# ConvGLU gate chunks and Mamba-2 convolution chunks projected in token rows and turned through HBM

## The chip, the cores and the metric

The kernel runs on one core of one Trainium2 chip. The metric is the device time of one execution in microseconds; lower is better. The time before is the median of three runs. The engines that matter are TensorE (PE, with its weight loads as PEld), VectorE (DVE), ScalarE (ACT) and GpSimd (POOL); SyncE (SP) and GpSimd also issue the transfers.

## The reference, cut to what matters

One layer over 256 tokens with a width of 2048, all in float32. Each sub-layer normalises its input and adds its result to the residual.

```python
proj = u @ w_in                                  # HGRN2, z, xbc, dt and two output gates
xbc = silu(causal_dwconv(xbc_raw, conv_w, conv_b))      # kernel width 4, 8 groups of 256+128+128 channels
xs, bm, cm = split(xbc)                          # then the Mamba-2 scan, gated by silu(z), normed
merged = sigmoid(g_hg) * y_hg + sigmoid(g_m2) * y_m2    # then w_out
# cross-attention into 256 memory tokens
gate, up = split(u @ w_up)                       # 5632 channels each
gate = causal_dwconv(gate, conv_w, conv_b)       # kernel width 3
h = h + (gelu(gate) * up) @ w_down               # then a last RMSNorm
```

A causal convolution runs along the tokens, separately for each channel. It is therefore wanted with channels on the partitions and tokens along the free dimension.

## The kernel before, in words

Every weight matrix is streamed from HBM once, in pieces of 128 x 2048 float32 (1 MB). `order` (lines 87 to 107) lists the pieces in the order of their use. `weights()` (line 201) hands out the next piece, and before that it advances every generator in `background` by one step and sees to it that three pieces are on their way. `issue()` loads a piece through SyncE's queue and splits it by halves of 1024 columns: ScalarE rounds a half to `hi` (line 130) and VectorE forms the rest `lo` (line 131). `hi` and `lo` have five buffers each, `raw` three. Activations are held as hi and lo parts side by side too, so a product is three matmuls: hi by hi, hi by lo, lo by hi.

There are two ways to use a piece.

- `project` (line 238) makes a chunk of 128 output channels for all 256 tokens. The weight is the stationary operand. For each of the 16 blocks of the inner dimension there is one matmul of `hi` over 512 columns (both parts of the activation) and one of `lo` over 256 columns, 32 matmuls for 1 MB. The result has channels on the partitions in two parts, which `join` (line 261) adds: a ScalarE copy out of PSUM and a VectorE sum.
- `project_tok` (line 245) makes 512 output channels for all tokens from four pieces. The activation is the stationary operand, and 24 matmuls of 512 columns use 1 MB. The result has tokens on the partitions, in two PSUM banks of 128 tokens each.

PSUM has four banks for these results (`pj`), two for `lev` and two for `misc`.

Results in token rows are turned by VectorE and HBM: VectorE transposes squares of 32 x 32 (`V.transpose`), `to_squares` (line 307) writes the four partition blocks to HBM with four GpSimd transfers, and one more transfer reads them back with channels on the partitions. The tokens then stand in another order, which `in_order` (line 323) undoes as a view.

Work that is not a projection runs in generators. Each `yield` ends a step, and a step belongs to one piece of weights. Their matmuls keep their place in the program order (`mm`, line 80); other instructions are placed by the scheduler of the tile framework when their operands and buffers are free. A tile name has a fixed number of buffers, and a new tile waits until an old one of that name has had its last use.

The parts around the change:

- Mamba-2, `m2_project` (line 715) and `m2_scan` (line 733). For each of eight groups four chunks are projected with `project(s2)`, joined into `raw` (name `t`, one buffer), and convolved by VectorE in four instructions into `sz` (two buffers). The scan of the group is then put in the background; it pauses one step (even group) or three (odd), applies SiLU, turns x, computes the decays, the product of B and C, the output, the gating and the norm, and writes the group's rows of `ym`. Every second group also has a gate projection of four pieces ahead of it (`m2_gates`).
- The feed-forward stage (lines 1047 to 1081). `values()` projects four chunks of `up` in token rows and turns them (`ut`, two buffers of four chunks). It runs four chunks ahead of the gate. Each of the 44 gate chunks is projected with `project(u3)`, joined, multiplied by the norm factor `r_f`, convolved in three instructions, put through Gelu, multiplied by `r_f` and by the turned value, and split into `hid[c]`. ScalarE's queue carries 16 small transfers of the residual in between.
- The down projection (from line 1090) uses seven matmul blocks in place of eight for some pieces, for which VectorE and ScalarE prepare sums of weights (`seven_forms`) and of inputs (`input_forms`).

Of the kernel before, what the change touches and what calls it, by code (L numbers as in the profile page):

```python
# [9 lines left out]
F32 = mybir.dt.float32  # L10
# [4 lines left out]
ALU = mybir.AluOpType  # L15
# [4 lines left out]
P = 128  # L20
T = 256
D = 2048
# [20 lines left out]
NS = 6  # L43

# [20 lines left out]
def hybrid_trunk(ctx, tc, xT, memT, par, cst, msk, w_k0, w_ka, w_va, w_hg, w_hv, w_hog, w_ghg, w_bhg, w_dt,  # L65
                 w_z, w_m2, w_gm2, w_bm2, w_out, w_q, w_o, w_ug, w_uv, w_dn, fin_g, outT):
    nc = tc.nc
# [125 lines left out]
    def pause(n):  # L193
        for _ in range(n):
            yield True
# [149 lines left out]
    def pc(name, i=0, n=1):  # L345
        o, _ = PCOLS[name]
        return par_t[:, o + i:o + i + n]
# [356 lines left out]
    def m2_chunk(g, i):  # L704
        return 2 * g + i if i < 2 else (16 + g if i == 2 else 24 + g)
# [9 lines left out]
    def m2_project(g):  # L715
        sz = mp.tile([P, 4, T], F32, name="sz", bufs=2)
        cb = mp.tile([P, 4, T], F32, name="vc", bufs=2)
        nc.sync.dma_start(out=cb, in_=cum_d[4 * g:4 * g + 4, :].partition_broadcast(P))
        for i in range(4):
            c = m2_chunk(g, i)  # L720
            ps = project(s2)
            raw = mp.tile([P, T], F32, name="t", bufs=1)
            join(mp, ps, raw)
            o = sz[:, i, :]
            V.tensor_scalar(out=o, in0=raw, scalar1=pc("m2_cw", 4 * c + 3), scalar2=pc("m2_cb", c),
                            op0=ALU.mult, op1=ALU.add)
            for s in range(1, 4):
                V.scalar_tensor_tensor(out=o[:, s:T], in0=raw[:, 0:T - s],  # L728
                                       scalar=pc("m2_cw", 4 * c + 3 - s), in1=o[:, s:T],
                                       op0=ALU.mult, op1=ALU.add)  # L730
        return sz, cb

    def m2_scan(g, sz, cb, zt):
        yield from pause(1 + 2 * (g % 2) if g else 0)

# [310 lines left out]

    def values():

        yq = fu.tile([P, 1024], F32, name="yq", bufs=1)
        for q, ps in enumerate(project_tok(u3)):  # L1050
            V.transpose(out=yq.rearrange("p (n q r) -> p q n r", q=2, r=B)[:, q],  # L1051
                        in_=ps.rearrange("p (n c) -> p n c", c=B))
        yd = to_squares(yq, 16, "u_d")
        ut = fu.tile([P, 4, T], F32, name="ut", bufs=2)
        G.dma_start(out=ut, in_=yd.rearrange("(j p) t -> p j t", p=P))
        return ut

    uts = [values()]
    for c in range(KF):
        if c % 4 == 0 and c + 4 < KF:  # L1060
            uts.append(values())
        if c % 2 == 0 and 4 <= c < 36:
            b, n = (c - 4) // 4, (c - 4) // 2 % 2 * (D // 2)
            nc.scalar.dma_start(
                out=rows_d[b * B:(b + 1) * B, n:n + D // 2].rearrange("i (n c) -> i n c", c=B),
                in_=h2_sq[:, n // B:n // B + D // 2 // B, b * B:(b + 1) * B])
        ps = project(u3)
        g = fu.tile([P, T], F32, name="g", bufs=1)
        join(fu, ps, g)
        V.tensor_tensor(out=g, in0=g, in1=r_f, op=ALU.mult)  # L1070
        gc = fu.tile([P, T], F32, name="gc", bufs=2)
# [6 lines left out]
        V.tensor_tensor(out=gc, in0=gc, in1=r_f, op=ALU.mult)  # L1078
        gv = gc.rearrange("p (q b t) -> p q b t", q=2, t=B)
        V.tensor_tensor(out=gv, in0=gv, in1=in_order(uts[c // 4][:, c % 4, :]), op=ALU.mult)  # L1080
        split(hid[c], gc)
    fx.close()

# [169 lines left out]
def _layout(inp):  # L1253
# [5 lines left out]
    swap = np.arange(D).reshape(GROUPS, 2, P // B, B).transpose(0, 2, 1, 3).ravel()  # L1259
    xs = _cols(cut(10240, 2048)).reshape(GROUPS, 2, P, 2048)  # L1260
    b = _cols(cut(12288, 1024))[:, None]
    c = _cols(cut(13312, 1024))[:, None]
    dt = np.zeros((D, P), f)
# [3 lines left out]
    k0 = ka[:NS].reshape(NS, P, KD // 2, 2, P).transpose(2, 1, 3, 0, 4)  # L1267
    up = inp["ffn_w_up"][0]
    out = _cols(inp["w_out"][0])
# [10 lines left out]
    def put(name, a):  # L1280
# [34 lines left out]
        "w_bhg": _toks(inp["w_branch_hg"][0]), "w_dt": _cols(dt),  # L1315
        "w_z": _toks(cut(8192, 2048)[:, swap]), "w_m2": np.concatenate([xs, b, c], 1), "w_gm2": _toks(cut(16416, 2048)),
        "w_bm2": _toks(inp["w_branch_m2"][0]), "w_out": out,
        "w_q": _cols(inp["xa_wq"][0]), "w_o": _cols(inp["xa_wo"][0]),
        "w_ug": _cols(up[:, :FF]), "w_uv": _toks(up[:, FF:]),
        "w_dn": np.ascontiguousarray(dn.transpose(0, 1, 3, 2, 4)).reshape(2, KF // 2, P, 2048),  # L1320
# [20 lines left out]
```

## Time and profile before

| | |
|---|---|
| median of three runs | 2229.68 us (2229.58 to 2229.78) |
| the profiled execution | 2230.02 us |
| its span, first to last instruction | 2228.3 us |
| mean granted TensorE clock | 0.998 |
| moved from and to HBM | 445.20 MB read, 25.20 MB written |

Busy time by stretch of the span, in us:

| stretch | what runs | TensorE | VectorE | ScalarE | GpSimd |
|---|---|---|---|---|---|
| 0 to 170 | memory keys, norms | 167.88 | 125.31 | 109.48 | 1.25 |
| 170 to 548 | HGRN2 | 378.00 | 320.09 | 274.27 | 40.77 |
| 548 to 711 | first Mamba-2 group, HGRN2 branch | 163.00 | 87.50 | 81.31 | 6.35 |
| 711 to 995 | Mamba-2 groups | 284.00 | 224.57 | 192.61 | 64.00 |
| 995 to 1132 | gates, Mamba-2 branch | 137.00 | 84.22 | 65.34 | 24.38 |
| 1132 to 1220 | output projection | 88.00 | 63.57 | 52.97 | 0.00 |
| 1220 to 1418 | cross-attention | 198.00 | 128.71 | 111.93 | 12.20 |
| 1418 to 1513 | its output projection | 94.83 | 71.98 | 54.67 | 0.00 |
| 1513 to 2000 | gate and up | 487.00 | 345.09 | 257.35 | 37.09 |
| 2000 to 2124 | down, first part | 124.00 | 109.96 | 69.64 | 0.00 |
| 2124 to 2229 | down, second part, last norm | 95.63 | 79.78 | 51.59 | 0.00 |

Busy time is the time covered by an engine's instructions. Matmuls overlap, so the cost of one is read from the distance between the starts of neighbours and not from its own duration. A row of a group of instructions gives line, engine, operation, output and inputs, count, then total busy time and mean duration of one in ns, then the idle time of the engine just before them and what ended it. A row of a timeline gives start and duration in us and, after `x`, how many instructions are merged in it.

### The profile page before, as it was taken

What the parts mean: (1) busy time and instruction counts of PE and PEld (TensorE: products, weight loads), DVE (VectorE), ACT (ScalarE), POOL (GpSimd) and SP (SyncE); (2) the same over time, 40 slices, a digit from 0 to 9 for tenths busy, and PEclk for the clock granted to TensorE, in tenths of its full rate; (3) what the DMA queues carried; (4) which work ended last, traced back from release to release, by engine and by line L of the source; (5) the groups of instructions that cost most, each with busy time, mean ns of one, the idle gap of its engine ahead of it and who ended that gap; (6) DMA issues with size and microseconds to landing.
All of it is one profiled execution on the core that took longest, in us unless ns stands there. A gap on an engine that the chain in (4) does not pass through costs nothing.

```text
span 2228.3 us, 32921 instructions
## 1 busy us (share of the span) xinstructions
PE 2217.3 (100%) x12620; PEld 1890.7 (85%) x12620; DVE 1640.8 (74%) x2660; ACT 1321.2 (59%) x2056; POOL 186.0 (8%) x314
## 2 busy tenths in 40 slices
PE   9999999999999999999999999999999999999998
PEld 8888888888888888888888888888888888888887
DVE  8858888887645779874676766675776776699887
ACT  7567777776545577665456655554554555465554
POOL 0000100110000122220200010001000100100000
PEclk9999999999999999999999999999999999999999
DMA  8655555555655667766676654578666666655654
GB/s 307 235 187 195 184 181 181 182 186 189 228 189 201 225 234 236 229 213 219 228 247 217 219 203 174 180 226 250 214 210 211 225 214 218 213 200 211 220 205 161
DMA packets 100270, 470.45 MB, mean 211 GB/s; under 512 B 29424, under 2 KB 34064, under 8 KB 51088
## 3 DMA queue, kind: packets, MB, share of 16 engines
q1 hardware_dynamic: 69600, 432.36, 54.8%
q0 software_dynamic: 13584, 33.57, 5.3%
q10 hardware_dynamic: 16928, 2.42, 0.6%
q8 instruction: 99, 1.62, 0.3%
q14 instruction: 59, 0.48, 0.1%
HBM read 445.20 MB, written 25.20 MB: 211 GB/s over the span
## 4 chain that ended last, share of the span: by engine, by line
PE 99%; DMA 0%; ACT 0%; SPq 0%; DVE 0%; issue 0%; DVEq 0%; ACTq 0%
PE proj L82 90%; PE misc L82 5%; PE lev L82 4%; DMA raw<-in_w_k 0%; ACT misc L1204 0%; DVE h L1202 0%; PE lev L869 0%; SPq L402 0%; ACT hi L386 0%; SPq L401 0%; DVE c L1221 0%; SPq L405 0%; DVEq L1337 0%; ACT jt L263 0%; PE misc L697 0%
## 5 line engine op out<-in xcount | busy, mean ns | idle before, releaser
L131 DVE TENSOR_TENSOR lo<-raw,hi 128x1024 fp32r<-128x1024 f32 x738 | 896.5, 1222 | 458.8 <-ACT hi L130 425.9
L130 ACT CAST hi<-raw 128x1024 fp32r<-128x1024 f32 x737 | 771.9, 1051 | 546.5 <-PE proj L82 513.0
L82 PE MATMUL proj<-hi,s 128*128 128x512 f32 x2922 | 913.6, 390 | 0.0
L82 PE MATMUL proj<-s,hi 128*128 128x512 f32 x2736 | 645.1, 391 | 1.1 <-ACT hi L386 1.1
L82 PEld LDWEIGHTS proj<-hi,s 128*128 128x128 f32 x2922 | 548.4, 188 | 114.4 <-issue 0.7
L82 PEld LDWEIGHTS proj<-s,hi 128*128 128x128 f32 x2736 | 506.5, 188 | 101.8 <-ACT hi L386 1.6
L82 PE MATMUL proj<-lo,s 128*128 128x512 f32 x1461 | 568.8, 389 | 0.0
L82 PEld LDWEIGHTS proj<-s,lo 128*128 128x128 f32 x2736 | 345.3, 191 | 11.3 <-ACT s L278 0.8
L82 PE MATMUL proj<-s,lo 128*128 128x256 f32 x2736 | 351.6, 283 | 0.2 <-ACT s L278 0.2
L82 PEld LDWEIGHTS proj<-lo,s 128*128 128x128 f32 x1461 | 274.4, 188 | 55.7
L312 POOL DMA_DIRECT2D x_d<-yq x120 | 69.9, 589 | 372.2 <-DVE yq L320 365.6
L165 ACT CAST hi<-raw 128x1024 fp32r<-128x1024 f32 (+1 forms) x56 | 52.1, 944 | 55.0 <-DVE raw L174 35.1
L263 ACT COPY jt<-proj 128x256 f32<-128x256 f32 x123 | 45.6, 371 | 57.5 <-PE proj L82 56.8
L312 POOL DMA_DIRECT2D u_d<-yq x44 | 28.6, 656 | 535.9 <-DVE yq L1051 342.6
L312 POOL DMA_DIRECT2D y_d<-yq x64 | 35.1, 555 | 384.1 <-DVE sm L618 263.1
L166 DVE TENSOR_TENSOR lo<-raw,hi 128x1024 fp32r<-128x1024 f32 (+1 forms) x56 | 60.2, 1088 | 6.9 <-ACT hi L165 6.2
L1074 DVE SCALAR_TENSOR_TENSOR gc<-g,par_t,gc 128x255 f32<-128x255 f32 x88 | 42.4, 482 | 8.7 <-ACT gc L1072 6.0
L728 DVE SCALAR_TENSOR_TENSOR sz<-t,par_t,sz 128x255 f32<-128x255 f32 (+2 forms) x96 | 45.6, 475 | 1.4
L1072 ACT ACTIVATE gc<-g,par_t 128x256 f32<-128x256 f32 x44 | 26.4, 601 | 20.9 <-DVE g L1070 20.9
L82 PE MATMUL proj<-hi,ha 128*128 128x512 f32 x104 | 36.6, 389 | 0.0
L572 DVE TENSOR_TENSOR e<-e,kq 128x256 f32<-128x256 f32 x96 | 34.4, 418 | 0.0
L559 DVE TENSOR_TENSOR e<-bb 128x256 f32<-128x256 f32 x96 | 33.8, 419 | 0.1
(315 smaller groups left out, 1801.3 us busy)
## 6 DMA issues: line engine op xcount, KB each, us to landing
raw<-in_w_uv SPq DMA_DIRECT2D x44, 1024.0 KB, 4.9
raw<-in_w_ug SPq DMA_DIRECT2D x44, 1024.0 KB, 4.8
raw<-in_w_dn SPq DMA_DIRECT2D x44, 1024.0 KB, 4.8
raw<-in_w_hg SPq DMA_DIRECT2D x32, 1024.0 KB, 4.8
raw<-in_w_m SPq DMA_DIRECT2D x32, 1024.0 KB, 5.0
raw<-in_w_hv SPq DMA_DIRECT2D x16, 1024.0 KB, 4.9
raw<-in_w_hog SPq DMA_DIRECT2D x16, 1024.0 KB, 4.8
raw<-in_w_ghg SPq DMA_DIRECT2D x16, 1024.0 KB, 4.8
```

Of the source, the lines that this page charges most:

```text
L82: ins = PE.matmul(*args, **kwargs)
L130: S.copy(out=hi[:, c - a:d - a], in_=raw[:, c:d])
L131: V.tensor_tensor(out=lo[:, c - a:d - a], in0=raw[:, c:d], in1=hi[:, c - a:d - a].bitcast(F32), op=ALU.subtract)
L165: S.copy(out=hi[:, 0:d - c], in_=raw[:, c:d])
L166: V.tensor_tensor(out=lo[:, 0:d - c], in0=raw[:, c:d], in1=hi[:, 0:d - c].bitcast(F32), op=ALU.subtract)
L263: S.copy(out=tmp, in_=ps[:, T:2 * T])
L312: G.dma_start(out=yd.rearrange("(n i) (b f) -> b i n f", i=B, b=P // B)[b], in_=yq[b * B:(b + 1) * B, :].rearrange("i (n f) -> i n f", n=n))
L559: V.tensor_tensor(out=lev[hw].rearrange("p (n c i) -> p n c i", c=2, i=hw), in0=free(bb, 0, [(2 * hw, nb), (T + hw, 2), (1, hw)]), in1=fre ...
L572: V.tensor_tensor(out=ev, in0=ev, in1=free(kq, 0, [(2 * hw, nb), (T + hw, 2), (1, hw)]), op=ALU.mult)
L728: V.scalar_tensor_tensor(out=o[:, s:T], in0=raw[:, 0:T - s], scalar=pc("m2_cw", 4 * c + 3 - s), in1=o[:, s:T], op0=ALU.mult, op1=ALU.add)
L1072: S.activation(out=gc, in_=g, func=AF.Identity, bias=pc("f_cb", c), scale=pc("f_cw", 3 * c + 2))
L1074: V.scalar_tensor_tensor(out=gc[:, s:T], in0=g[:, 0:T - s], scalar=pc("f_cw", 3 * c + 2 - s), in1=gc[:, s:T], op0=ALU.mult, op1=ALU.add)
```

## The change

Both convolved projections go over to token rows.

In the feed-forward stage ten rounds each project 512 value channels and 512 gate channels with `project_tok`, transpose both and write both to HBM (`rows_out`). A generator `four` reads gates and values of a round back by four transfers, one step after it was put in the background, pauses three steps and then handles one chunk in each step. The chunk's first product reads the turned gate through `in_order` in place of the join. The last four gate chunks stay in the direct form, and their four value chunks now use it too: each pair is two `project` calls with a join each. The order of the weights is changed to match (ten times four value and four gate pieces, then four pairs).

In the Mamba-2 part groups 1 to 6 project their four chunks with one `project_tok`, transpose them, write them to HBM and read them back into `sz` with GpSimd transfers. `m2_scan` for these groups first pauses three steps, then copies each chunk out of `sz` into `raw` in token order on ScalarE and convolves it back into `sz`, two chunks a step, then pauses one step (even group) or three (odd). Group 0 and group 7 stay direct; group 7 pauses six steps in place of three. The host's weight layouts follow; they are not shown.

```diff
+FG = 10
...
-    for p in range(-1, KF // 4):
-        order += [w_uv[p + 1, i] for i in range(4) if p + 1 < KF // 4]
-        order += [w_ug[4 * p + i] for i in range(4) if p >= 0]
+    order += [w[p, i] for p in range(FG) for w in (w_uv, w_ug) for i in range(4)]
+    order += [w_ut[c, i] for c in range(KF - 4 * FG) for i in range(2)]
...
         nc.sync.dma_start(out=cb, in_=cum_d[4 * g:4 * g + 4, :].partition_broadcast(P))
+        if 0 < g < GROUPS - 1:
+            pss = project_tok(s2)
+            for j in range(2):
+                yq = mp.tile([P, 2 * T], F32, name="yq", bufs=2)
+                for q in range(2):
+                    V.transpose(out=yq.rearrange("p (n q r) -> p q n r", q=2, r=B)[:, q],
+                                in_=pss[q][:, j * T:(j + 1) * T].rearrange("p (n c) -> p n c", c=B))
+                yd = to_squares(yq, T // B, "r_d")
+                G.dma_start(out=sz[:, 2 * j:2 * j + 2, :], in_=yd.rearrange("(i p) t -> p i t", p=P))
+            return sz, cb
         for i in range(4):
-            c = m2_chunk(g, i)
             ps = project(s2)
             raw = mp.tile([P, T], F32, name="t", bufs=1)
             join(mp, ps, raw)
...
+            convolve(g, sz, i, raw)
...
     def m2_scan(g, sz, cb, zt):
-        yield from pause(1 + 2 * (g % 2) if g else 0)
+        if 0 < g < GROUPS - 1:
+            yield from pause(3)
+            for i in range(4):
+                raw = mp.tile([P, T], F32, name="t", bufs=1)
+                S.copy(out=raw.rearrange("p (q b t) -> p q b t", q=2, t=B), in_=in_order(sz[:, i, :]))
+                convolve(g, sz, i, raw)
+                if i % 2:
+                    yield True
+        yield from pause((0, 1, 3, 6)[0 if g == 0 else 3 if g + 1 == GROUPS else 1 + g % 2])
...
+    def four(p, vd, gd):
+        yield True
+        vts, gts = [], []
+        for j in range(2):
+            for name, d, ts in (("gt", gd, gts), ("vt", vd, vts)):
+                t = fu.tile([P, 2, T], F32, name=name, bufs=2)
+                G.dma_start(out=t, in_=d[j * T:(j + 1) * T, :].rearrange("(i p) t -> p i t", p=P))
+                ts.append(t)
+        yield from pause(3)
+        for i in range(4):
+            c = 4 * p + i
+            g = fu.tile([P, T], F32, name="g", bufs=1)
+            V.tensor_tensor(out=token_order(g), in0=in_order(gts[i // 2][:, i % 2, :]),
+                            in1=token_order(r_f), op=ALU.mult)
+            gc = gated(c, g)
+            V.tensor_tensor(out=token_order(gc), in0=token_order(gc),
+                            in1=in_order(vts[i // 2][:, i % 2, :]), op=ALU.mult)
+            split(hid[c], gc)
+            if i < 3:
+                yield True
...
+    for p in range(FG):
+        residual_rows(2 * p)
+        vd = rows_out("v_d")
+        residual_rows(2 * p + 1)
+        background.append(four(p, vd, rows_out("g_d")))
+    for c in range(4 * FG, KF):
+        ps = project(u3)
+        g = fu.tile([P, T], F32, name="g", bufs=1)
+        join(fu, ps, g)
+        V.tensor_tensor(out=g, in0=g, in1=r_f, op=ALU.mult)
+        gc = gated(c, g)
+        ps = project(u3)
+        up = fu.tile([P, T], F32, name="yq", bufs=1)
+        join(fu, ps, up)
+        V.tensor_tensor(out=gc, in0=gc, in1=up, op=ALU.mult)
         split(hid[c], gc)
+    drain()
```

`rows_out` is `values` without the load: `project_tok(u3)`, two transposes, `to_squares`. `gated` holds the convolution, Gelu and the product with `r_f` as they were; `convolve` holds the four instructions that were in `m2_project`; `residual_rows` holds the residual's transfers, two for each round from the second to the ninth.

More of the change, by code (lines that the diff above doesn't have):

```diff
@@ L65, in hybrid_trunk @@
 def hybrid_trunk(ctx, tc, xT, memT, par, cst, msk, w_k0, w_ka, w_va, w_hg, w_hv, w_hog, w_ghg, w_bhg, w_dt,
[L66 removed]
+                 w_z, w_m2, w_gm2, w_bm2, w_out, w_q, w_o, w_ug, w_uv, w_ut, w_dn, fin_g, outT):
     nc = tc.nc
@@ L723, in m2_project, with convolve @@
             join(mp, ps, raw)
[L724 to L730, printed above, removed]
-        return sz, cb
-    def m2_scan(g, sz, cb, zt):
-        yield from pause(1 + 2 * (g % 2) if g else 0)
+            convolve(g, sz, i, raw)
+        return sz, cb
+    def convolve(g, sz, i, raw):
+        c = m2_chunk(g, i)
+        o = sz[:, i, :]
+        V.tensor_scalar(out=o, in0=raw, scalar1=pc("m2_cw", 4 * c + 3), scalar2=pc("m2_cb", c),
+                        op0=ALU.mult, op1=ALU.add)
+        for s in range(1, 4):
+            V.scalar_tensor_tensor(out=o[:, s:T], in0=raw[:, 0:T - s],
+                                   scalar=pc("m2_cw", 4 * c + 3 - s), in1=o[:, s:T],
+                                   op0=ALU.mult, op1=ALU.add)
+    def m2_scan(g, sz, cb, zt):
+        if 0 < g < GROUPS - 1:
[7 more added lines that the diff above has]
+        yield from pause((0, 1, 3, 6)[0 if g == 0 else 3 if g + 1 == GROUPS else 1 + g % 2])
         xc = mp.tile([P, 2 * T], F32, name=("w", "ql")[g % 2], bufs=1)
@@ L1045, in hybrid_trunk, with rows_out @@
     h2_sq = h2_d.rearrange("n (b i) t -> i (n b) t", i=B)
-    def values():
+    def rows_out(name):
         yq = fu.tile([P, 1024], F32, name="yq", bufs=1)
@@ L1052, in values, with token_order, gated @@
                         in_=ps.rearrange("p (n c) -> p n c", c=B))
[L1053 to L1070, printed above, removed]
+        return to_squares(yq, 16, name)
+    def token_order(x):
+        return x.rearrange("p (q b t) -> p q b t", q=2, t=B)
+    def gated(c, g):
         gc = fu.tile([P, T], F32, name="gc", bufs=2)
@@ L1078, in hybrid_trunk, with residual_rows @@
         V.tensor_tensor(out=gc, in0=gc, in1=r_f, op=ALU.mult)
-        gv = gc.rearrange("p (q b t) -> p q b t", q=2, t=B)
-        V.tensor_tensor(out=gv, in0=gv, in1=in_order(uts[c // 4][:, c % 4, :]), op=ALU.mult)
+        return gc
+    def four(p, vd, gd):
[18 more added lines that the diff above has]
+                yield True
+    def residual_rows(i):
+        if 2 <= i < 18:
+            b, n = (i - 2) // 2, i % 2 * (D // 2)
+            nc.scalar.dma_start(
+                out=rows_d[b * B:(b + 1) * B, n:n + D // 2].rearrange("i (n c) -> i n c", c=B),
+                in_=h2_sq[:, n // B:n // B + D // 2 // B, b * B:(b + 1) * B])
+    for p in range(FG):
[13 more added lines that the diff above has]
+        V.tensor_tensor(out=gc, in0=gc, in1=up, op=ALU.mult)
         split(hid[c], gc)
+    drain()
     fx.close()
@@ L1259, in _layout @@
     swap = np.arange(D).reshape(GROUPS, 2, P // B, B).transpose(0, 2, 1, 3).ravel()
-    xs = _cols(cut(10240, 2048)).reshape(GROUPS, 2, P, 2048)
-    b = _cols(cut(12288, 1024))[:, None]
-    c = _cols(cut(13312, 1024))[:, None]
+    xbc = np.concatenate([cut(10240, 2048).reshape(D, GROUPS, 256),
+                          cut(12288, 1024).reshape(D, GROUPS, P),
+                          cut(13312, 1024).reshape(D, GROUPS, P)], 2).reshape(D, GROUPS * 512)
+    m2 = _toks(xbc)
+    for g in (0, GROUPS - 1):
+        m2[g] = _cols(xbc[:, g * 512:(g + 1) * 512])
     dt = np.zeros((D, P), f)
@@ L1267, in _layout @@
     k0 = ka[:NS].reshape(NS, P, KD // 2, 2, P).transpose(2, 1, 3, 0, 4)
-    up = inp["ffn_w_up"][0]
+    up, up_to = inp["ffn_w_up"][0], FG * 512
     out = _cols(inp["w_out"][0])
```

5 lines of the change are left out of this document (3 added, 2 removed).

## The prediction

> **What bounds the kernel now.** I read the page's busy times first, then the chain that ended last, then what TensorE waited for.
>
> ```profile
> PE 2217.3 (100%) x12620; PEld 1890.7 (85%) x12620; DVE 1640.8 (74%) x2660; ACT 1321.2 (59%) x2056; POOL 186.0 (8%) x314
> PE 99%; DMA 0%; ACT 0%; SPq 0%; DVE 0%; issue 0%; DVEq 0%; ACTq 0%
> ```
> ```profile
> PE proj L82 <- ACT hi L386: 1.1, 2, 0.8
> PE misc L82 <- POOL eps_t L343: 1.0, 1, 1.0
> PE proj L82 <- ACT s L278: 0.2, 1, 0.2
> ```
> TensorE is 99% of the chain, and its waits for other engines add up to 2.3 us, all of them small. So the time is the sum of its matmuls, and a change gains only by making that sum shorter and loses only by making TensorE wait. Where the other engines wait, they wait for it:
>
> ```profile
> ACT hi L130 <- PE proj L82: 513.0, 400, 3.4
> DVE lo L131 <- ACT hi L130: 425.9, 347, 4.4
> ```
> ScalarE casts a weight half (`hi`) as soon as TensorE gives a buffer back, VectorE makes `lo` behind it.
>
> **What the two forms cost on TensorE.** The timeline of TensorE over one period of the feed-forward stage, four gate chunks (`project`) and four megabytes of values (`project_tok`, elided):
>
> ```profile
> 1548.64 2.08 PE L82 MATMUL proj<-s,lo 128*128 128x256 f32 x16
> 1550.56 7.44 PE L82 MATMUL proj<-s,hi 128*128 128x512 f32 x32
> 1557.84 4.00 PE L82 MATMUL proj<-s,lo 128*128 128x256 f32 x32
> 1561.67 7.44 PE L82 MATMUL proj<-s,hi 128*128 128x512 f32 x32
> 1568.95 2.08 PE L82 MATMUL proj<-s,lo 128*128 128x256 f32 x16
> 1570.86 0.40 PE L82 MATMUL proj<-hi,s 128*128 128x512 f32 x1
> ...
> 1592.65 2.08 PE L82 MATMUL proj<-s,lo 128*128 128x256 f32 x16
> ```
> By starts, four gate chunks take 1570.86 - 1548.64 = 22.22 us, four value weights 1592.65 - 1570.86 = 21.79 us. Both stream the same number of columns: `project` 16 x 512 + 16 x 256 for each megabyte, `project_tok` 24 x 512. The difference sits in the 256-wide matmuls: 1561.67 - 1557.84 = 3.83 us for 32 is 0.120 us each, while a 512-wide one of the token form takes 21.79 / 96 = 0.227, so its half would be 0.1135. Sixteen times 0.006 is most of the 0.1075 us by which one megabyte is cheaper in token rows.
>
> [...] The rows above have 0.107, and I take the rows.
>
> **What is moved between the forms.** 40 gate chunks and 24 convolved chunks (six groups of four) go from `project` to `project_tok`. The last four value chunks go the other way, since the remainder of four has a gate and a value weight each in `project`. Net 64 - 4 = 60 megabytes: 60 x 0.1075 = 6.45 us less TensorE work. Other rows bound it: the chain's pieces of one weight,
>
> ```profile
> 881.93 5.47 PE proj L82 x24
> 887.40 1.50 PE misc L82 x16
> ...
> 916.69 0.65 PE misc L82 x4
> 917.34 5.56 PE proj L82 x32
> 922.90 1.50 PE misc L82 x16
> ```
> give 5.56 - 5.47 = 0.09 (5.4 us), and the down stage's 24-matmul weight at 0.68 us for three, 5.44, gives 0.12 (7.2 us):
>
> ```profile
> 2016.16 0.68 PE lev L82 x3
> ```
> **Other work in the feed-forward stage.** The groups of instructions, by shape:
>
> ```profile
> L131 DVE TENSOR_TENSOR lo<-raw,hi 128x1024 fp32r<-128x1024 f32 x738 | 896.5, 1222 | 458.8 <-ACT hi L130 425.9 <-PE proj L82 28.1 <-ACT sq L290 0.4
> L264 DVE TENSOR_TENSOR g<-proj,jt 128x256 f32<-128x256 f32 x44 | 18.4, 418 | 0.1
> L1051 DVE STREAM_TRANSPOSE yq<-proj 128x512 f32<-128x512 f32 x22 | 14.5, 694 | 2.4 <-PE proj L82 2.4
> L320 DVE STREAM_TRANSPOSE yq<-lf 128x256 f32<-128x256 f32 x16 | 7.1, 445 | 2.3 <-ACT lf L645 1.5
> L312 POOL DMA_DIRECT2D u_d<-yq x44 | 28.6, 656 | 535.9 <-DVE yq L1051 342.6 <-ACT hi L130 192.4 <-issue 0.9
> L1055 POOL DMA_DIRECT2D ut<-u_d x11 | 8.5, 773 | 44.2 <-DMA u_d<-yq 44.2
> ```
> For each four gate chunks VectorE loses four joins (4 x 0.418 = 1.67 us) and gains two transposes (2 x 0.694 = 1.39), ScalarE loses four copies, and the product with r_f reads turned rows at the price of the value product, which reads so today. VectorE is level; the windows say it has room:
>
> ```profile
> 1592.65:1636.66 44.01, 44.01 (x226) 37.70 (x225) 31.18 (x47) 23.09 (x32) 3.38 (x5) 1.00 0.62 215
> 853.40:924.40 71.00, 71.00 (x393) 60.87 (x393) 59.02 (x101) 49.59 (x82) 18.29 (x30) 1.00 0.73 237
> 1989.10:2063.00 73.90, 73.90 (x327) 60.87 (x327) 70.25 (x115) 40.50 (x55) 0.00 (x0) 1.00 0.55 200
> ```
> (after the length: TensorE, weight loads, VectorE, ScalarE, GpSimd, clock, DMA share, GB/s). GpSimd's queue gets 8 writes instead of 4 and 4 loads instead of 1: 8 x 0.656 + 4 x 0.773 = 8.3 us of 43.6. The gate's new way through HBM must be ready when `four` multiplies:
>
> ```profile
> u_d<-yq POOLq DMA_DIRECT2D x44, 128.0 KB, 4.0
> ut<-u_d POOLq DMA_DIRECT2D x11, 512.0 KB, 5.4
> ```
> Transposes 1.4, four writes 2.6, landing 4.0, four loads 3.1, landing 5.4: 16.5 us after the last matmul. The first chunk comes on the fifth step, four weights or 21.8 us later. That covers it with 5.3 us left. Behind it lies a second cover: `hi` and `lo` have five half buffers each, so a half is made when the half five places ahead is given back, four halves (10.9 us) before use, less cast (about 1.05) and subtraction (1.22): 8.6 us that ScalarE or VectorE may be late before TensorE sees it. Extra HBM traffic is 1 MB beside 8 MB of weights; at a DMA share of 0.62 I cost it at nothing, with that cover.
>
> **The end of the feed-forward stage.** The last `four` runs beside the direct remainder. Packed tightly, a 256-wide product takes 0.335 us and a subtraction 1.14, by starts:
>
> ```profile
> 1967.97 0.41 DVE L1080 TENSOR_TENSOR gc<-gc,ut 128x256 f32<-128x256 f32 x1
> 1968.31 0.42 DVE L1070 TENSOR_TENSOR g<-g,r_f 128x256 f32<-128x256 f32 x1
> 1968.64 1.22 DVE L131 TENSOR_TENSOR lo<-raw,hi 128x1024 fp32r<-128x1024 f32 x1
> 1969.78 0.42 DVE L279 TENSOR_TENSOR h<-gc,h 128x256 fp32r<-128x256 f32 x1
> 1970.11 0.99 DVE L1074 SCALAR_TENSOR_TENSOR gc<-g,par_t,gc 128x255 f32<-128x255 f32 x2
> ```
> In the last four weights VectorE gets 8 x 1.14 for `lo`, four turned chunks of 4 x 0.335 + 0.91 (the pair above less the overlap with the next), two direct gates of 1.92 and two direct values of 1.0: 23.9 us against 22.2 on TensorE. It enters the down stage 1.7 us behind, plus a last value of 1.0, 2.7 in all; today it enters with a whole last gate chunk of 2.6. The down stage is the tight place (70.25 of 73.9 above), and there
>
> ```profile
> 2000.26 1.06 ACT L130 CAST hi<-raw 128x1024 fp32r<-128x1024 f32 x1 [2.10 <-PE proj L82]
> ...
> 2001.34 1.23 DVE L131 TENSOR_TENSOR lo<-raw,hi 128x1024 fp32r<-128x1024 f32 x1 [0.31 <-ACT hi L130]
> ```
> the half for a weight begun near 2005 is ready at 2002.6, 2.4 us ahead. Equal backlogs mean no wait; bounds 0 and 2.7, I take 0.3.
>
> **The Mamba-2 groups.** Per group VectorE loses four joins (1.67) and gains four 256-wide transposes (1.78); ScalarE's copy stays a copy. GpSimd gets 8 writes and 2 loads, at the prices above 6.8 us of a 35.5 us group in which it is busy for 9.1. The raw rows come three steps (16.3 us) later, and the scan's first SiLU moves from step 2 or 4 to step 7 or 9. A group's `sz` is held until its B-C product, now at step 11 (even) or 13 (odd). For groups in token rows that costs nothing: the next user writes it by DMA after step 12. Group 7 stays direct and is projected in steps 9 to 12 of group 5, whose `sz` it needs. Its first convolution must wait for step 13, and it holds the only `t` buffer, so the other joins wait too, and so do group 6's convolutions. Three of the four PSUM banks stay full when the first output gate starts and needs two: its second bank comes free after one convolution and one join (three steps at L1074's 0.46 and two products, 2.0 us) behind the 0.65 us product, while TensorE has between 0.7 us (three matmuls) and 2.7 us (all twelve of that weight for the other bank) to do. So 0 to 2 us. Then in four weights (21.8 us, with the 0.65 and 1.50 us scan products above 23.9) VectorE has eight convolutions (13.6), three joins (1.0), 9.1 of `lo` and an estimated 5.9 of scan work, as products and transposes of the sizes above: 29.6 us, a backlog of 5.7 inside the 8.6 us cover. Bounds 0 and 5.7 (not below: TensorE has no waits there to lose); I take 0.5, nearest to the rows of before, in which VectorE's load never makes TensorE wait.
>
> **Sum.** Profiled execution 2230.02 (span 2228.3 and 1.7 around it), less 6.45, plus 0.8 of waits: 2224.4. The median of the runs is 0.34 lower than the profiled one, so 2224.0 us.
>
> **Rivals.**
> (a) The saving is eaten. Group 7's held-back convolutions expose their backlog (up to 5.7 us) and the entry to the down stage its 2.7: 6.45 saved, 2 to 8.4 lost. With 4.5 lost, 2227.7. For it: VectorE at 70.25 of 73.9 and a burst with more work than time. Against it: 8.6 us of cover.
> (b) Slower. The turned rows come too late, and the in-order queues of ScalarE and VectorE stand at them with the casts behind. Place: ScalarE's copy out of `sz` and VectorE's first product of each turned gate chunk, 16 groups of work. It decides once rows are later than margin plus cover (5.3 + 8.6 us in the feed-forward stage; in the mixer the second half of `sz`, by the same rows two round trips of 2.6 + 4.0 + 0.8 and a landing of 5.4, 20.2 us against four weights, so 1.6 + 8.6). Each microsecond beyond costs 16; 0.7 us beyond in every group cancels the gain and crosses into slower at 10.9. At 1.2 us it gives 19.2 - 6.45, 2242.4. For it: GpSimd waits for landings in order, 44.2 us for eleven loads today. Against it: the margins.
> [...]
>
> [...]
>
> That the matmuls do not change form cannot be, as the program fixes it.
>
> **How the numbers follow.** About 0.2% (4.5 us) is what a measurement can tell from none, so faster means below 2225.2: waits of at most 2 us. Chances: forecast 0.60, (a) 0.25, (c) 0.03, (b) 0.12. The forecast's own range is 2222.3 to 2225.2, with the bounds 5.4 and 7.2 of the saving. For 8 in 10 it runs from 2221.5 to 2231, which takes in (c) and (a) to its upper bound, and leaves out (b). Faster 0.60, same 0.28, slower 0.12.
>
> **What would show it.** The count of 256-wide matmuls,
>
> ```profile
> L82 PE MATMUL proj<-s,lo 128*128 128x256 f32 x2736 | 351.6, 283 | 0.2 <-ACT s L278 0.2
> ```
> falls by 60 x 16 to 1776. A feed-forward period shrinks from 44.01 to 43.6, two Mamba-2 groups from 71.0 to 70.15. TensorE's waits stay under 4 us; if they name `lo`, `hi` or a PSUM evacuation near group 7's end or at the start of the down stage, (a) is right; if they recur in each group behind DMA landings, (b). Wrong altogether would be a token-row weight of more than 5.5 us where nothing waits.

## The result and the profile after

The changed kernel takes 2247.07 us (median of 4 runs, 2244.04 to 2248.83); the kernel before took 2229.73 us beside it. The ratio is 1.0076 with a 95% interval of 1.0064 to 1.0089: slower by 17.3 us, where 5.7 us faster was forecast. The profiled execution took 2248.83 us with a span of 2247.0.

The page of the changed kernel: busy times, the 256-wide matmuls, and the piece of the chain that covers the feed-forward stage.

```profile
PE 2219.6 (99%) x12140; PEld 1869.5 (83%) x12140; DVE 1638.9 (73%) x2642; ACT 1318.1 (59%) x2026; POOL 265.2 (12%) x439
...
L84 PE MATMUL proj<-s,lo 128*128 128x256 f32 x1776 | 230.0, 284 | 7.0 <-ACT sg L713 7.0
...
1536.57 482.44 PE proj L84 x2188
```

The same piece in the kernel before:

```profile
1513.40 486.82 PE proj L82 x2476
```

The program does what it says: 1776 matmuls of 256 columns, as forecast. The feed-forward piece is 4.38 us shorter. But it begins 23.2 us later (1536.57 against 1513.40), so everything that was lost was lost ahead of it. TensorE's waits in the changed kernel (total, times, longest):

```profile
PE proj L84 <- ACT sg L713: 7.0, 1, 7.0
PE misc L84 <- DVE bb L800: 3.9, 2, 3.7
PE proj L84 <- DVE yq L726: 3.2, 1, 3.2
PE proj L84 <- ACT s L846: 3.2, 1, 3.2
```

Before, all its waits came to 2.3 us. These four sum to 17.3, and the timeline puts every one into the Mamba-2 stage:

```profile
887.62 1.11 PE L84 MATMUL misc<-e,bb 128*64 128x256 f32 x2 [3.71 <-DVE bb L800]
...
931.11 1.44 PE L84 MATMUL proj<-s,lo 128*128 128x256 f32 x5 [7.05 <-ACT sg L713]
...
955.01 2.29 PE L84 MATMUL proj<-s,hi 128*128 128x512 f32 x6 [3.23 <-DVE yq L726]
...
1097.16 0.50 PE L84 MATMUL proj<-hi,s 128*128 128x512 f32 x1 [3.22 <-ACT s L846]
```

The scans of groups 1 and 2 pass without a wait; the first wait is at the output product of group 3. A second loss comes behind the waits. The windows of TensorE alone show it (length, busy time, granted clock, DMA share, GB/s):

```profile
887.60:889.00 1.40, 1.38 (x3) 0.50 0.93 187
889.00:891.00 2.00, 2.00 (x6) 0.53 1.01 420
891.00:893.00 2.00, 2.00 (x17) 1.00 0.71 170
...
924.00:931.00 7.00, 0.06 (x1) 0.82 0.54 198
...
932.00:934.00 2.00, 1.99 (x12) 0.50 0.02 4
934.00:936.00 2.00, 2.00 (x15) 0.69 0.00 0
...
955.00:957.00 2.00, 1.99 (x6) 0.68 0.82 291
957.00:959.00 2.00, 2.00 (x6) 0.50 0.65 133
...
1097.00:1101.00 4.00, 3.84 (x17) 1.00 0.13 16
```

Behind three of the four waits TensorE runs at half clock for some microseconds: about 3.4 us behind the first (887.5 to 890.9), about 6.8 us in and behind the second (928.4 to 935.2, the last 4.1 of them with work), and 3.4 behind the third (955.7 to 959.1). Behind the first, two matmuls of 512 columns take 0.85 us by their starts (890.11 - 889.26); ahead of it they take 0.45 (882.39 - 881.94). So about half of the time with work at that clock is lost, 5.5 us by estimate (half of 3.4 + 4.1 + 3.4). Waits and half clock make 22.8 us. Set against the start of the feed-forward piece, 23.2 us late where 2.6 early was forecast, 25.8 us were lost; 3 us of these I have not placed.

The length of a wait doesn't settle whether half clock follows: the clock was 0.50 behind a wait of 3.23 us (957 to 959) and 1.00 behind one of 3.22 (1097 to 1101), and in a kernel below it was 0.50 behind one of 2.23.

How the first wait comes about shows when group 2 (in order) is set beside group 4. VectorE transposes the projected rows out of PSUM (L726), GpSimd loads them back (L729), ScalarE copies them for the convolution (L753):

```profile
778.32 1.44 DVE L726 STREAM_TRANSPOSE yq<-proj 128x256 f32<-128x256 f32 x4
784.56 0.72 POOL L729 DMA_DIRECT2D sz<-r_d  x1 [1.37 <-DMA r_d<-yq]
791.10 0.41 ACT L753 COPY t<-sz 128x256 f32<-128x256 f32 x1 [0.35 <-DMA sz<-r_d]
791.97 0.72 POOL L729 DMA_DIRECT2D sz<-r_d  x1 [3.33 <-DMA r_d<-yq]
...
852.38 0.78 DVE L726 STREAM_TRANSPOSE yq<-proj 128x256 f32<-128x256 f32 x2 [0.34 <-DMA x_d<-yq]
860.57 0.78 DVE L726 STREAM_TRANSPOSE yq<-proj 128x256 f32<-128x256 f32 x2 [0.39 <-DMA x_d<-yq]
868.09 0.72 POOL L729 DMA_DIRECT2D sz<-r_d  x1 [4.04 <-issue]
874.37 0.41 ACT L753 COPY t<-sz 128x256 f32<-128x256 f32 x1 [4.54 <-DMA sz<-r_d]
874.68 1.05 ACT L131 CAST hi<-raw 128x1024 fp32r<-128x1024 f32 x1
874.81 0.41 DVE L741 TENSOR_SCALAR sz<-t,par_t 128x256 f32<-128x256 f32 x1 [3.73 <-ACT t L753]
875.28 0.72 POOL L729 DMA_DIRECT2D sz<-r_d  x1 [4.16 <-DMA r_d<-yq]
882.61 0.41 ACT L753 COPY t<-sz 128x256 f32<-128x256 f32 x1 [3.23 <-DVE sz L744]
...
887.15 0.42 DVE L800 TENSOR_TENSOR bb<-kq,dt_tok 128x256 f32<-128x256 f32 x1
```

In group 2 all four transposes go at once, and the second load is issued 13.7 us behind the first of them. In group 4 the transposes wait for a `yq` buffer, which a write of a scan (`x_d`) still reads; the second pair comes 8 us after the first, and the second load 22.9 us behind the first transpose. So the copy stands 4.54 us at a load that has not landed, with a weight cast behind it; VectorE stands 3.73 us at the copy, and the third copy stands 3.23 us for the one buffer `t`. These late convolutions of group 4 stand in VectorE's order ahead of work of groups 2 and 3, so group 3's product `bb`, which TensorE wants at 884, comes only at 887.15.

### The profile page after: what moved, and what is told of

Read it like the earlier page. It is cut to its first block, busy times and chain, and to the rows that moved or that the text cites. A ratio compares the mean times of both kernels' runs of the same rounds, so it can differ in the third digit from the quotient of the medians.

```text
span 2247.0 us, 32184 instructions
## 1 busy us (share of the span) xinstructions
PE 2219.6 (99%) x12140; PEld 1869.5 (83%) x12140; DVE 1638.9 (73%) x2642; ACT 1318.1 (59%) x2026; POOL 265.2 (12%) x439
## 4 chain that ended last, share of the span: by engine, by line
PE 51%; DMA 0%; issue 0%; ACT 0%; DVE 0%; DVEq 0%; POOLq 0%
PE proj L84 45%; PE misc L84 4%; PE lev L84 3%; DMA yc<-x_d 0%; ACT misc L1260 0%; PE lev L892 0%; DVE h L1258 0%; DVE c L1277 0%; DMA x_d<-yq 0%; ACT s L846 0%; DVEq L1398 0%; ACT r L1267 0%; ACT r L1268 0%; DVE r L1266 0%; POOLq L840 0%
## 5 line engine op out<-in xcount | busy, mean ns | idle before, releaser
L84 PE MATMUL proj<-hi,s 128*128 128x512 f32 x3882 | 1209.1, 390 | 3.3 <-ACT s L846 3.2
L84 PEld LDWEIGHTS proj<-hi,s 128*128 128x128 f32 x3882 | 729.0, 188 | 156.3 <-ACT s L846 3.6
L84 PE MATMUL proj<-lo,s 128*128 128x512 f32 x1941 | 757.0, 390 | 0.0
L84 PEld LDWEIGHTS proj<-lo,s 128*128 128x128 f32 x1941 | 364.6, 188 | 76.5 <-issue 1.8
L84 PE MATMUL proj<-s,hi 128*128 128x512 f32 x1776 | 423.1, 392 | 3.6 <-DVE yq L726 3.2
L84 PEld LDWEIGHTS proj<-s,hi 128*128 128x128 f32 x1776 | 329.6, 189 | 69.5 <-issue 3.6
L84 PEld LDWEIGHTS proj<-s,lo 128*128 128x128 f32 x1776 | 225.0, 192 | 14.9 <-ACT sg L713 7.5
L84 PE MATMUL proj<-s,lo 128*128 128x256 f32 x1776 | 230.0, 284 | 7.0 <-ACT sg L713 7.0
L313 POOL DMA_DIRECT2D v_d<-yq x40 | 25.9, 655 | 320.5 <-ACT hi L131 192.3
L313 POOL DMA_DIRECT2D r_d<-yq x48 | 28.0, 588 | 54.7 <-DVE yq L726 43.6
```

The costliest lines, as they stand in the source:

```text
L84: ins = PE.matmul(*args, **kwargs)
L313: G.dma_start(out=yd.rearrange("(n i) (b f) -> b i n f", i=B, b=P // B)[b], in_=yq[b * B:(b + 1) * B, :].rearrange("i (n f) -> i n f", n=n))
```

## The experiments

All were timed beside the kernel before. Where a time without any loss is named, it is 2229.7 less 0.11 us for each megabyte of token rows: 2223.1 for the whole change (2229.7 - 4.0 - 24 x 0.11).

**Which half of the change.** One kernel has only the feed-forward part of the diff, another only the Mamba-2 part.

```diff
 # feed-forward only: m2_project, m2_scan and w_m2 as before
 # Mamba-2 only: the feed-forward loop, w_ug and w_uv as before
```

> The feed-forward part of the change alone, with the Mamba-2 part of before. Both theories put the whole loss into the Mamba-2 stage, so both expect 36 net chunks x 0.1075 = 3.9 us less than before, 2225.8 us, TensorE's waits as in before (2.3 us) and a feed-forward period of 43.6 us. A rival that puts part of the loss on the turned gates expects 2229 or more and waits behind vt or gt.

Measured: 2225.79 us (2225.46 to 2226.70), ratio 0.9981 (0.9971 to 0.9990), TensorE's waits 2.5 us.

> The Mamba-2 part alone, with the feed-forward part of before. Both theories expect the loss of the changed kernel without its feed-forward gain: about 2247 + 4 = 2251 us (2246 to 2256), with TensorE waits of 14 to 22 us, all between the first Mamba-2 group and the last product of that stage, and the clock at half after some of them.

Measured: 2252.85 us (2250.49 to 2255.23), ratio 1.0101 (1.0086 to 1.0116), with the same four waits (7.0, 3.9, 3.2, 2.4). The halves nearly add up: against the kernel before beside them (2230.14 us) the feed-forward part brings 4.4 us and the Mamba-2 part loses 22.7, together 18.4 us, where the whole change lost 17.3.

**GpSimd's queue.** First the new transfers are moved off it, then two idle round trips are put onto it in the kernel before.

```diff
-yd = to_squares(yq, T // B, "r_d")
-G.dma_start(out=sz[:, 2 * j:2 * j + 2, :], ...)
+yd = to_squares(yq, T // B, "r_d", nc.sync)
+nc.sync.dma_start(out=sz[:, 2 * j:2 * j + 2, :], ...)
```

> The changed kernel with the writes and loads of the turned raw rows on SyncE's queue; the other three round trips of a group stay with GpSimd. Queue theory (five in-order round trips a group fill GpSimd's queue, the scans slip later, ScalarE and VectorE stand in order at late landings): the waits of TensorE fall under 5 us and the time to 2223 to 2230. Holding theory (later scans keep sz, the z rows and the transpose buffers too long, whatever the queue): waits stay above 12 us, 2240 or more.

Measured: 2236.76 us (2234.86 to 2238.35), ratio 1.0029 (1.0018 to 1.0039). Ten of the 24 us come back, neither forecast. Of the four waits of the changed kernel only 1.5 us at `s` and 0.7 us at `bb` are left, and a new one of 3.0 us names a weight cast. ScalarE's timeline there:

```profile
821.84 0.40 ACT L753 COPY t<-sz 128x256 f32<-128x256 f32 x1 [2.10 <-DVE sz L744]
822.15 3.88 ACT L131 CAST hi<-raw 128x1024 fp32r<-128x1024 f32 x4
```

Four casts stand in line behind a copy that waits for the buffer `t`, not for a row.

```diff
 # the kernel before, at the end of m2_project, groups 1 to 6
+for j in range(2):
+    yd = turned(mp, <two convolved chunks of sz>, T // B, "r_d")
+    dz = mp.tile([P, T], F32, name="ec", bufs=1)
+    G.dma_start(out=dz, in_=yd[0:P])
```

> Before, with two more round trips a group on GpSimd for groups 1 to 6: the convolved chunks are transposed by VectorE (two of 128x512), written in four pieces each and read back (half of it, 128 KB) into a tile that nobody uses. The matmuls, their forms and the steps of the scans are those of before, so nothing is held longer by design. Queue theory: the scans' own loads come late and TensorE waits, 5 to 20 us more than before, 2235 to 2250. Holding theory: 2229.7 within 1.5.

Measured: 2231.88 us (2230.86 to 2233.09), ratio 1.0007 (0.9998 to 1.0017). This is just above the holding forecast and far below the other. A longer queue whose rows nobody waits for costs about 2 us, though its writes hold `yq` buffers too, so the occupied queue alone is not the cause. It does make the scans later: the output product of one group follows its B-C product by 13.2 us (967.06 - 953.82), where it was 6.2 or 6.3 in every group before.

```profile
953.82 0.81 PE L82 MATMUL misc<-sz 128*128 128x256 f32 x4
967.06 1.81 PE L82 MATMUL misc<-e,bb 128*64 128x256 f32 x16
```

TensorE doesn't wait there. Its own order is another: by the records 55 projection matmuls stand between these two products, where the kernel before has 24 or 32 in every group. So the matmuls of a scan don't keep their distance from one program to the next. In the changed kernel the count is 25 in groups 1 and 2 and 52 to 114 from group 3 on; with only groups 5 and 6 in token rows (below) it is 58 and 114 in groups 6 and 7, without a wait, so lateness can be hidden in this way.

**A second buffer for the raw rows.**

```diff
-raw = mp.tile([P, T], F32, name="t", bufs=1)
+raw = mp.tile([P, T], F32, name=("t", "ec")[i % 2], bufs=1)
```

> The changed kernel, but the raw rows copied out of `sz` alternate between two buffers (`t` and the idle `ec`) instead of one, so that ScalarE's next copy need not wait for VectorE's four products on the last. If the handing to and fro of the one buffer makes ScalarE and VectorE late (one-buffer theory), the waits of 3.7 and 7.0 us fall and the time is 2236 to 2242 us. If the copies wait for rows that have not landed, or the later scans hold banks and buffers (late-rows theory), a second buffer helps nothing: 2245 to 2249 us.

Measured: 2240.34 us (2239.46 to 2244.81), ratio 1.0051 (1.0036 to 1.0066). The one-buffer theory's number. The waits in group 3 and at `yq` are gone and two later ones stay; the one at `bb` is now at group 7's output product, where the changed kernel waits 0.15 us (the profiled execution, 2244.81 us, is the slowest of the four):

```profile
PE proj L84 <- ACT sg L713: 6.7, 1, 6.7
PE misc L84 <- DVE bb L800: 3.6, 1, 3.6
PE proj L84 <- ACT s L846: 3.0, 1, 3.0
```

**Convolutions a step later, scans a step earlier.**

```diff
 # later convolutions, same scan
-yield from pause(3)        ...  pause((0, 1, 3, 6)[...])
+yield from pause(4)        ...  pause((0, 0, 2, 6)[...])
 # two raw buffers, earlier scans
-pause((0, 1, 3, 6)[...])
+pause((0, 0, 2, 5)[...])
```

> The changed kernel with the convolutions of groups 1 to 6 one step (5.5 us) later and the scan's first SiLU at the same step as in the changed kernel: the pause ahead of the copies is 4 instead of 3, the one behind them 0 or 2 instead of 1 or 3. If the copies stand at rows that have not landed (late-rows theory), one step more lets them land, the wait behind `bb` (3.7 us) goes and the time is 2237 to 2244 us. If the trouble is that all of a group's later work is bunched and pushed back (holding theory), it stays or grows: 2246 to 2254 us.

Measured: 2244.5 us (2240.66 to 2247.25), ratio 1.0068 (1.0051 to 1.0085), between the two forecasts. The wait at `bb` falls to 0.9 us and the one at `sg` to 2.4, but the one at `yq` rises to 4.4. Giving the rows more time to land goes with a shorter wait at `bb`; the median doesn't tell the theories apart.

> The changed kernel with two buffers for the raw rows (as in the run before of that kind, 2240.3 us) and every scan of groups 1 to 7 one step (5.5 us) earlier behind its convolutions: pauses 0, 2 and 5 instead of 1, 3 and 6. What is left of TensorE's waits there names the copy of group 6's `z` rows into `sg` (6.7 us), behind a late scan that still reads the buffer. If it is the scans' lateness that holds `sg` and the PSUM banks (holding theory), that wait goes and the time is 2229 to 2235 us. If the waits come from work that is bunched wherever it stands (load theory), they only move: 2238 to 2243 us.

Measured: 2236.37 us (2235.08 to 2238.02), ratio 1.0029 (1.0017 to 1.0042), again between. The 6.7 us at `sg` are gone, as the holding theory says: in the changed kernel, where this wait is 7.0 us, ScalarE's copy out of PSUM into `sg` starts at 930.49, behind a scan's last product that reads `sg` (`kq<-bb,sg`, 928.41). With the earlier scans the longest wait is one for a transpose out of PSUM (4.5 us).

A version with group 7's pause cut from six steps to three, which was to test rival (a) directly, deadlocks, so it has no time.

**How many groups.** Only the last groups before group 7 are in token rows; the others are direct.

```diff
-if 0 < g < GROUPS - 1:
+if 4 < g < GROUPS - 1:     # groups 5 and 6; 3 < g: 4 to 6; 2 < g: 3 to 6
```

> The changed kernel with groups 1 to 4 direct as before the change and only groups 5 and 6 in token rows, group 7 behind them with its pause of 6; the feed-forward part as changed. Without any loss it would take 2229.7 - 4.0 (feed-forward, as measured by that part alone) - 8 x 0.11 = 2224.9 us. If the lateness grows from one token-row group to the next (growth theory), two groups stay within the cover: 2225 to 2227 us. If each token-row group costs the same, two sixths of 26 us stay: 2233 to 2235 us. If the handing over to the direct group 7 is what costs, that is all still there, 3 to 7 us of waits: 2228 to 2232 us.

Measured: 2226.10 us (2225.67 to 2228.87), ratio 0.9985 (0.9975 to 0.9994). No wait over 0.6 us but the 1.0 at `eps_t`, which stood before the change: two groups cost next to nothing (1.2 us above the 2224.9 without any loss), and the direct group 7 behind them shows no wait of its own.

> The changed kernel with only groups 4 to 6 in token rows (one raw buffer), so that the scan of group 3, which frees the buffer for group 6's `z` rows, is direct and early. Without any loss 2229.7 - 4.0 - 12 x 0.11 = 2224.4 us. Growth theory: a third group in a row brings a first wait of about 3 us and 3.4 us at half clock, 2227 to 2231 us. Position theory: nothing waits, 2224 to 2226.5 us.

Measured: 2230.91 us (2229.67 to 2234.38), ratio 1.0007 (0.9998 to 1.0016). The number is the growth theory's, but not its place: the wait (3.2 us) is at the last rows of group 7. GpSimd and ScalarE there, with two groups and no wait:

```profile
1062.94 2.33 POOL L313 DMA_DIRECT2D x_d<-yq  x4 [16.69 <-DVE yq L321]
1069.84 0.72 POOL L840 DMA_DIRECT2D yc<-x_d  x1 [4.58 <-issue]
1073.50 0.91 ACT L846 ACTIVATE s<-yc,par_t 128x256 fp32r<-128x256 f32 x2 [0.59 <-DMA yc<-x_d]
```

and with three groups:

```profile
1061.09 2.32 POOL L313 DMA_DIRECT2D x_d<-yq  x4 [14.28 <-DVE yq L321]
1069.94 0.72 POOL L840 DMA_DIRECT2D yc<-x_d  x1 [6.53 <-DMA x_d<-yq]
1075.30 0.91 ACT L846 ACTIVATE s<-yc,par_t 128x256 fp32r<-128x256 f32 x2 [4.23 <-DMA yc<-x_d]
```

The writes are issued 1.9 us earlier with three groups, but GpSimd stands 6.53 us behind them rather than 4.58, so the load is issued at the same time in both. It then takes longer to land, 5.3 us against 3.6. And TensorE asks for these rows at 1072.7 with three groups, while with two it has no wait there although ScalarE starts on them only at 1073.50: the two programs also differ in the order of TensorE's work. In the kernel before, the load was issued some 46 us earlier; the later scans have used that up:

```profile
1023.50 0.72 POOL L817 DMA_DIRECT2D yc<-x_d  x1 [4.78 <-DMA x_d<-yq]
```

> The changed kernel with only groups 3 to 6 in token rows (one raw buffer, pauses as changed), groups 1 and 2 direct. Without any loss 2229.7 - 4.0 - 16 x 0.11 = 2224.0 us. Growth theory (lateness adds up from group to group, and shows from the third on): waits of 3 to 8 us and some half clock, 2228 to 2236 us. Position theory (the loss belongs to group 6's `z` rows, which need the buffer that group 3's scan reads, late because group 3 is in token rows): the 7.0 and the 3.2 us wait with their half clock are there in full, 2236 to 2242 us.

Measured: 2227.47 us (2226.23 to 2234.37), ratio 0.9993 (0.9984 to 1.0003); the profiled execution, 2232.2 us, has a wait of 4.1 us at `bb`. Position theory falls. The median is under even the growth forecast, and under that of three groups: the loss is no steady function of the number of groups.

> Groups 3 to 6 in token rows with two buffers for the raw rows. Growth theory: with the second buffer the four groups stay nearly within the cover, 2224 to 2228 us. Position theory: the wait at `sg` remains as in the six-group run with two buffers, 2233 to 2239 us.

Measured: 2232.85 us (2228.65 to 2236.65), ratio 1.0013 (1.0004 to 1.0023). Missed: the second buffer that gained 6.7 us with six groups loses 5.4 with four. The profiled execution is the fastest of the ten (2228.65 us), with a wait of 2.0 us at group 7's last rows; where the others lose more isn't shown.

**Which cost of the way through HBM.** The loads into `sz` read weights that lie ready in HBM, so the mixer works on other numbers; then the writes are left out too.

```diff
-G.dma_start(out=sz[...], in_=yd.rearrange("(i p) t -> p i t", p=P))
+G.dma_start(out=sz[...], in_=w_m2[g, j][:, 0:2 * T].rearrange("p (i t) -> p i t", t=T))
 # and in the second kernel
-yd = to_squares(yq, T // B, "r_d")
```

> The changed kernel, but the loads into `sz` read rows that lie ready in HBM (weights, so the convolutions work on other numbers and the mixer's result is not the reference's); the writes of the raw rows stay, on the same queue. GpSimd then doesn't stand for the landing of those writes, and the rows are in `sz` early. Late-rows theory (the copies stand at rows that have not landed): 2224 to 2234 us. Holding theory (what costs is that scans start three steps later and hold `sz`, `sg`, `yq` and PSUM banks for longer): 2240 to 2248 us.

Measured: 2238.58 us (2236.51 to 2240.42), ratio 1.0039 (1.0024 to 1.0054), between the two forecasts. TensorE's longest waits:

```profile
PE proj L84 <- DVE yq L726: 3.2, 1, 3.2
PE misc L84 <- DVE bb L800: 2.8, 2, 2.3
PE proj L84 <- ACT s L846: 1.5, 1, 1.5
```

> As the run with ready rows, and the writes of the raw rows are left out as well (the transposes into `yq` stay; the mixer's result is not the reference's), so that GpSimd's queue is as short as before the change but for 12 loads, and `yq` is free as soon as its transpose is done. Only the later scans are left of the change's cost in the Mamba-2 stage. Holding theory: 2238 to 2247 us. Late-rows theory: 2224 to 2230 us. If queue, rows and held `yq` buffers add up, with no single cause: 2226 to 2232 us here, and about half the loss in the run with ready rows.

Measured: 2231.12 us (2227.60 to 2231.82), ratio 1.0000 (0.9991 to 1.0010). The third forecast, that no single cause does it, is the one that holds here; of the loss, 8.5 of 24 us came back in the run with ready rows, where it expected about half:

```profile
PE misc L84 <- DVE e L795: 3.2, 1, 3.2
PE proj L84 <- ACT s L845: 1.4, 1, 1.4
```

The medians make a ladder: 2223.1 with no loss, 2231.1 with the later scans, the copies and loads of ready rows, 2238.6 with the writes on GpSimd's queue and in `yq`, 2247.1 with the rows read from those writes. Steps of 8.0, 7.5 and 8.5 us, in this order of removal; they are no fixed prices, since about the same writes cost 2 us in the kernel before, where the scans are early.

**The end of group 7, and a faster version.**

```diff
 # groups 5 and 6, and 3 to 6: scans one step earlier
-pause(0 if g == 0 else 6 if g + 1 == GROUPS else (1, 3)[g % 2])
+pause(0 if g == 0 else 5 if g + 1 == GROUPS else (1, 3)[g % 2] - (g >= 5))   # g >= 3
 # and: the product with the gate, group 7
-yield from pause(4 if g + 1 < GROUPS else 3)
+yield from pause(4 if g + 1 < GROUPS else 2)
```

> Groups 5 and 6 alone in token rows, as in the run that took 2226.1 us, with the scans of groups 5, 6 and 7 one step earlier (pauses 2, 0 and 5 instead of 3, 1 and 6). If group 7's last rows stand on an edge (the runs with three and with four groups differ by whether the write in front of them lands in 4.6 or 6.5 us), one step takes them off it and the time is 2225 to 2226 us with little spread. If something else spreads the runs, 2226 to 2229 us as it was.

Measured: 2233.43 us (2229.55 to 2236.49), ratio 1.0015 (1.0006 to 1.0025). Missed on both sides: an earlier scan made it 7 us slower, with a wait of 3.9 us at group 7's rows.

> Groups 3 to 6 in token rows with the scans of groups 3 to 7 one step earlier. Holding theory: the 4.1 us wait at the output product of group 3 and the half clock behind it go, 2224 to 2226.5 us. Late-rows theory: the SiLU now stands right behind convolutions of rows that come no earlier, so that wait stays or grows, 2227 to 2234 us.

Measured: 2226.69 us (2225.95 to 2231.54), ratio 0.9988 (0.9979 to 0.9997). The time lies between the two forecasts. The 4.1 us wait at `bb` is 0.7 here, as the holding theory says.

> The changed kernel with the pause between group 7's load of `yt` and its product with the gate cut from 3 steps to 2, so that its last rows can be a step (5.4 us) earlier. End theory (group 7's last rows arrive when TensorE needs them, a wait of 3.2 us in the changed kernel and 3.2 or 3.9 in others): the wait at `s` goes and the time falls by 3 to 6 us, 2241 to 2244 us. If TensorE's later waits only take its place, 2245 to 2249 us.

Measured: 2246.28 us (2244.88 to 2248.53), ratio 1.0076 (1.0060 to 1.0093). The wait at `s` is 3.3 us as it was. The pause was not what set these rows, and the end theory, as I put it, falls.

> Groups 5 and 6 in token rows (the run of 2226.1 us) with the same pause of group 7 at 2 instead of 3. End theory: 2224.9 to 2226 us and no run above 2227. Otherwise 2226 to 2230 us.

Measured: 2226.37 us (2225.72 to 2231.46), ratio 0.9986 (0.9976 to 0.9995). The end theory misses here too: the time is as it was, with one execution of 2231.46.

> Groups 3 to 6 in token rows with scans one step earlier (the run of 2226.7 us), and the same pause of group 7 at 2 instead of 3. If the end was what spread its runs from 2226.0 to 2231.5 us, the time is 2224.0 to 2226.0 us with a spread under 2 us; without any loss it would be 2224.0. If VectorE now stands at rows of `yt` that have not landed, 2226 to 2230 us.

Measured: 2226.66 us (2225.84 to 2240.37), ratio 0.9993 (0.9980 to 1.0005). The spread didn't shrink. The profiled execution is the 2240.37, and it shows what a bad one of these runs is made of:

```profile
PE misc L84 <- DVE bb L800: 8.6, 2, 4.8
PE misc L84 <- DVE e L796: 1.3, 1, 1.3
```

One and the same program takes 2226 or 2240 us. That such waits come up in one execution and not in another, by a landing that takes longer, is my reading: no trace of a fast execution of this program shows it.

No version with Mamba-2 groups in token rows was faster than the feed-forward part alone, 2225.79 us; groups 5 and 6 with it (2226.10) come out level with it, though 0.9 us of matmul time, by estimate (8 x 0.11), is saved there.

## Why the prediction was wrong

**The price of the forms: right.** 36 MB net in the feed-forward stage at 0.1075 us are 3.9 us; the feed-forward part alone brought 4.4, and the piece of the chain is 4.38 us shorter: 0.12 us for each megabyte, the upper of the prediction's bounds. In the Mamba-2 stage the price shows where nothing waits: from group 1 to group 3 the B-C products in the run with ready rows lie 70.10 us apart, in the kernel before 71.01, against a forecast of 70.15.

```profile
801.16 0.81 PE L84 MATMUL misc<-sz 128*128 128x256 f32 x4
...
871.26 0.81 PE L84 MATMUL misc<-sz 128*128 128x256 f32 x4
```

In the changed kernel they lie 70.91 us apart (871.29 - 800.38), though TensorE doesn't wait there either. Its output product of group 2 is split up among the projection's matmuls, eight at 842.35 and eight at 844.05, where the run with ready rows has sixteen at 842.42. That this takes the 0.8 us is not shown, but they are among the 3 us that I have not placed above.

Rival (c), that the two forms cost nearly the same, is out: no run shows the small difference it rests on, and the runs have 0.12 us for each megabyte.

**The feed-forward stage and its end: right.** The margin and the cover held, and neither the stage nor the entry to the down stage shows a new wait: the feed-forward part alone has 2.5 us of waits, the kernel before 2.3. That half of rival (a) is out.

**The Mamba-2 groups: the step that failed.** It said 0.5 us where 24 were lost by the medians, and 25.8 in the profiled execution. Three sentences of it were wrong, and the ladder, in its order of removal, gives each about a third.

- "For groups in token rows that costs nothing": holding `sz`, and starting the scan five steps later, was costed by the next user of `sz` alone. The later scan also holds `sg`, into which ScalarE copies PSUM rows (TensorE's wait of 7.05 us), and the work of a group falls onto the queues of the next ones. With no writes, and loads of rows that lie ready, 8.0 us are still lost.
- "6.8 us of a 35.5 us group in which it is busy for 9.1" counted GpSimd's busy time. The queue goes in order, and in the changed kernel from 770 to 1000 it stood 42.0 us at landings of its own writes, up to 4.9 us at one; and the writes hold `yq`, of which the scans use the same two buffers. In group 4 the transposes out of PSUM waited for them, and the second load was issued 22.9 us behind the first transpose, where 13.7 was the time in group 2. Behind the later scans the writes make 7.5 us.
- The margin of "1.6 + 8.6" us against late rows took a group's two round trips as if alone, and the cover as whole in each group. In group 4 the copy stands 4.54 us at its load with a cast behind it. Rows that come from their writes, over rows that lie ready, make 8.5 us.

The prediction reckoned group by group from a fresh start; what the runs show adds up from group to group, since two groups cost next to nothing and six cost 24 us. How it adds up isn't settled: three groups came out slower than four, and a second buffer or an earlier scan helped in one arrangement and hurt in another.

**Rival (a)** had the right stage and the wrong mechanism. Group 7's held-back convolutions did not show as such: two groups ahead of a direct group 7 took 2226.1 us. The wait in group 7 is at its last rows, whose load is issued 67 us later than before (1090.60 against 1023.50). Its bound of 8.4 us lost was far too small.

**Rival (b)** was nearest, with 2242.4 us and with in-order queues that stand at turned rows, in the mixer. The chance of 0.12 came from the margins above. But its mechanism makes about a third of the loss, and it put the loss into 16 groups by equal parts, where the feed-forward stage shows none and groups 1 and 2 next to none. The half clock behind the waits, 5.5 us, was in no rival.

The lower end of the forecast's own range, 2222.3 us, comes out at 2222.5 by its bound of 7.2 (2229.7 - 7.2); nothing hangs on it.

**What stays open:** 3 of the 25.8 us; why the loss jumps about between close arrangements, where each edit also changes the order of the work on the engines, a part that no run separates from the edit; and whether all six groups could be hidden with more buffers for `yq` and `sg`, which was not tried.

## What to carry to other kernels

When a step is moved through a buffer or a queue, reckon the new way with everybody who uses that buffer and that queue, and follow it over several rounds of the loop: a margin that covers one round says little if each round hands its delay on. An engine that is busy for a third of the time can still have less room than that says, when it stands in order at landings: GpSimd was busy for 55.84 us of the 175 from 815 to 990, and stood at landings for another 30.5. And take such a change in parts: here the half with slack brought 4.4 us, and the other lost 22.7.

## What the runs showed of the hardware

A short wait of TensorE can cost more than its length: in the changed kernel the granted clock was 0.50 for 3.4 us behind waits of 3.71 and 3.23 us, and for 6.8 us in and behind one of 7.05. The shortest such wait is in the kernel with the Mamba-2 part alone, where TensorE waits 2.23 us for `bb` at 887.30:

```profile
887.40:889.00 1.60, 1.60 (x4) 0.50 0.79 230
...
891.00:893.00 2.00, 2.00 (x17) 1.00 0.58 125
```

It is not sure to come: behind 3.22 us at 1097 in the changed kernel the clock stayed at 1.00. And the way through HBM is not steady: in the kernels with two and with three groups, which differ little, GpSimd stood 4.58 or 6.53 us between four writes of the same rows and their load, and the load landed after 3.6 or 5.3 us.
